# Sliding-window attention by whole chunks: the order of scores, transposes and weighing, and the PSUM banks they use

## The chip, the cores and the metric

The kernel runs on one core of one Trainium2 chip. The metric is the device time of one execution in microseconds. The core's engines work side by side, each through its own instruction queue in order: TensorE (PE; its weight loads are shown apart as PEld), VectorE (DVE), ScalarE (ACT), GpSimd (POOL) and SyncE (SP), which issues most of the DMAs. Matmul results go to PSUM, which has eight banks of 2 KB for each of 128 partitions: one bank holds 128x512 numbers of 32 bits.

## The reference, cut to what matters

The reference computes one layer of a streaming encoder in float32, on 1024 prompt tokens and 64 sample tokens: a projection, retention and sliding-window attention side by side, their merging, cross attention to 256 memory tokens, and a feed-forward block. The change lies in the sliding-window attention. Queries come in chunks of 64; each chunk sees its own 64 keys and the 128 before them. There are 16 query heads and 2 heads of keys and values; each query head has a learned sink, which joins the softmax's denominator.

```python
def swa_attend(q, k, v, bias, sinks, valid):
    s = jnp.einsum('bnqhgd,bnkhd->bnhgqk', q, k, preferred_element_type=jnp.float32) * (SWA_HD ** -0.5)
    s = s + bias.astype(jnp.float32)
    if valid is not None:
        s = jnp.where(valid, s, NEG_INF)
    sink = sinks.astype(jnp.float32)[:, :, None, None]
    m = jnp.maximum(jnp.max(s, axis=-1, keepdims=True), sink)
    e = jnp.exp(s - m)
    p = e / (jnp.sum(e, axis=-1, keepdims=True) + jnp.exp(sink - m))
    return jnp.einsum('bnhgqk,bnkhd->bnqhgd', p.astype(v.dtype), v)
```

One other product of the layer is worked on at the same time: the retention branch's output product, `rms_norm(ret_o) * silu(ret_g)` times `w_ret_out`.

## The kernel before, in words

**Where the change lies.** The projections, the retention and the memory's keys and values come first (up to about 809 us of the profile's clock). Then `swa_phase` runs the attention over 17 chunks (16 of the prompt, one of the sample), from 809 to about 990 us; `merge_swa`, cross attention and the feed-forward block follow and are not touched.

**A chunk's steps.** A chunk c is worked on in two halves hf of eight query heads each. One half has four units (v, i): v is the head of keys and values, i one of two groups. Keys and queries of v=0 lie in partitions 0 to 63, those of v=1 in 64 to 127. `keys(c)` tells how many keys a chunk has: 64 for chunk 0, 128 for chunk 1, 192 for the others.
- `scores(c, hf)`: four matmuls (L972; eight records in the trace) that use half of PE's rows each, into one tile of two PSUM banks, "s", of which there is one. VectorE adds the bias and takes the minimum for each unit (L982, result `nm`), ScalarE takes the exponentials with their sums (L988) and the sinks' exponentials (`es`, L990), VectorE makes the denominators (L991) and reciprocals (L992), and POOL normalises: the first 128 keys in place in tile `t` (L994), the last 64 into tile `e` (L999).
- `turn(c, hf)`: in the first half, `values` transposes up to three blocks of 128 values on PE (L949) into one of the two PSUM banks "d" of the product below, and ScalarE copies each out (L951); a block once transposed is kept for the chunks that follow. Then four transposes of `t` (L1011) into the bank "pt0", copied out by ScalarE (L1015), and two of `e` (L1022) into the bank "pt1", copied out by VectorE (L1024).
- `weigh(c, hf)`: only in the second half, eight matmuls (L1035; sixteen records) of values by transposed weights, into the two banks "out". VectorE copies the result (L1039, `osb`), and every second chunk SP stores it.

**The work in between.** PE is kept busy by the retention's output product: `filler` yields half pieces of it. It first finishes the memory's values (four halves of 256 columns, operands `ms`; ScalarE takes each result out of bank "d", L1167) and then does 24 pieces of `w_ret_out` by `ret`, with 384, 384 or 320 columns. A half piece is twelve matmuls (L156 to L158: three for each of four blocks, since each float32 operand is split into a high and a low part). The splits are made by ScalarE (cast of the high part, L123) and VectorE (the low part, L124; L1120 for the first piece's operands, in `first_low`). `later_operands` loads and splits the retention output's second and third columns while the first pieces run; `marks` holds the `es` instructions that these casts and subtractions are set behind. VectorE multiplies each finished piece by its gate (L1196), and SP stores it.

**What sets the order.** The loop at L1047 emits, for each half, the weighing of the half before, the scores of the half two ahead, the transposes of this half, and then as many half pieces as `fill` names: none before the first step, six after the second, then 38 spread over 34 steps, and eight at the end. `in_order` (`issue_after(self.last_mm)`) sets each part behind the last matmul emitted, and so fixes PE's order; what the other engines do is put in order by a scheduler, which works from its own estimates of times. PSUM: "s" 2 banks, "pt0" 1, "pt1" 1, "out" 2, "d" 2, which is all eight.

Of the kernel before, what the change touches and what calls it, by code (L numbers as in the profile page):

```python
# [11 lines left out]
F32 = mybir.dt.float32  # L12
# [7 lines left out]
P = 128  # L20
# [16 lines left out]
NKEY = 192  # L37
# [72 lines left out]
class Kernel:  # L110
# [816 lines left out]
    def swa(self, ctx, fill):  # L927
        nc, tc, io = self.nc, self.tc, self.io
        if True:
# [26 lines left out]
            halves = [(c, hf) for c in range(17) for hf in range(2)]  # L956
# [7 lines left out]
            def scores(c, hf):  # L964
                ks, j0, nk = keys(c)
                if hf == 0 and c % 4 == 0 and 0 < c < 13:
                    self.load_queries(qTs, c + 4)
                qT = qTs[c // 4 % 2]
                pss = pw.tile([P, 2, 512], F32, tag="s", name="pss")
                for i in range(2):  # L970
                    for v in range(2):
                        self.last_mm = mm(pss[:, v, i * NKEY:i * NKEY + nk], qT[rows[v], 2 * hf + i, c % 4, :],  # L972
                                          kT[rows[v], ks:ks + nk], start=True, stop=True).ins
# [3 lines left out]
                ps = pss[:, :, :2 * NKEY].rearrange("p v (i n) -> p v i n", n=NKEY)  # L977
                bs = bias.rearrange("p (v h i) n -> p v h i n", v=2, h=2)
                nm = sw.tile([P, 2, 2], F32, tag="nm", name="nm")
                for v, i in units:  # L980
                    u = quad(self.minus)[:, v, i:i + 1]
                    nc.vector.tensor_tensor_reduce(t[:, v, i, :nk], ps[:, v, i, :nk], bs[:, v, hf, i, j0:], -0.125, u,  # L982
                                                   ALU.add, ALU.min, nm[:, v, i:i + 1])
# [19 lines left out]
            def turn(c, hf):  # L1003
                ks, j0, nk = keys(c)
                if hf == 0:
                    live[c] = [values(ks + k0) for k0 in ((0, 64, P) if nk == NKEY else (0,))]
                (t, e), vt = live.pop((c, hf)), live[c]
                n = min(P, nk)
                pp = pw.tile([P, 512], F32, tag="pt0", name="pp")
                for j, (v, i) in enumerate(units):  # L1010
                    self.last_mm = nc.tensor.transpose(pp[:n, j * P:(j + 1) * P], t[:, v, i, :n], self.ident).ins  # L1011
                if hf == 0:
                    live[c, "T"] = [self.pw2.tile([P, 2, 512], F32, tag="pT0", name="pT"), self.pw2.tile([P, 512], F32, tag="pT1", name="pT")]
                pT = live[c, "T"][0][:n]
                nc.scalar.copy(pT[:, :, hf * 256:(hf + 1) * 256], pp[:n, :].rearrange("p (v i) -> p v i", v=2))  # L1015
                cs = [slice(h * 256, (h + 1) * 256) for h in range(2)]
                parts = [[(h, v, vt[0][:n], pT[:, v, cs[h]]) for h in range(2) for v in range(2)]]
                if nk == NKEY:
                    pp = pw.tile([P, 512], F32, tag="pt1", name="pp")
                    for i in range(2):  # L1020
                        x = e[:, i].rearrange("p r k -> p (r k)")
                        self.last_mm = nc.tensor.transpose(pp[:, i * P:(i + 1) * P], x, self.ident).ins  # L1022
                    pT = live[c, "T"][1]
                    nc.vector.tensor_copy(pT[:, hf * 256:(hf + 1) * 256], pp[:, :256])  # L1024
                    parts.append([(h, r ^ h, vt[2 - r][rows[r]], pT[rows[r], cs[h]]) for h in range(2) for r in (h, 1 - h)])
                live[c, "parts"] = parts

            def weigh(c, hf):
                if hf == 0:
                    return  # L1030
                parts = live.pop((c, "parts"))
                po = pw.tile([P, 2, 512], F32, tag="out", name="pout")
# [14 lines left out]
            n = len(halves)  # L1047
            for i in range(-2, n):
                if i > 0:
                    self.in_order(lambda: weigh(*halves[i - 1]))  # L1050
                if i + 2 < n:
                    self.in_order(lambda: scores(*halves[i + 2]))
                if i >= 0:
                    self.in_order(lambda: turn(*halves[i]))
                for pieces in next(fill):
                    self.in_order(lambda: next(pieces, None))
                if i == -2:
                    with tc.high_priority(), tc.issue_after(self.last_operand):
                        self.tokens(vT, 1, "cvT")
                if i == 2:  # L1060
                    with tc.issue_after(self.last_operand):
                        self.load_queries(qTs, 4)
                if i == 8:
                    with tc.issue_after(self.last_operand):
                        keep()
            self.in_order(lambda: weigh(*halves[n - 1]))
            for pieces in next(fill):
                self.in_order(lambda: next(pieces, None))
# [765 lines left out]
```

## Time and profile before

| what | before |
|---|---|
| time, median of 3 runs (lowest, highest) | 2181.74 us (2180.3, 2183.03) |
| the profiled execution's own time | 2183.19 us |
| its span | 2181.1 us |
| mean granted clock of PE | 0.995 |
| PE busy, of the span | 2142.3 us (98%) |
| VectorE / ScalarE / POOL busy | 1553.4 / 876.4 / 651.7 us |
| PE busy in 826 to 870 us | 41.58 of 44.00 us |
| PE busy in 890 to 970 us | 80.00 of 80.00 us |

The busy time of PE is close to the span, so the table by itself does not tell what a change of order is worth: that depends on the few stretches in which PE waits, and on how quickly its matmuls follow one another. A row of the timeline holds the start and the duration of a group of like instructions in microseconds; in brackets stands the engine's idle time before it, and what ended that. Matmuls are pipelined: a row's duration is longer than the distance to the next row's start, and the distances are what counts.

### The profile page before, as it was taken

The page shows a single profiled execution, that of the slowest core. Times are in us where ns is not written, and L with a number is a line of the kernel's source. Part 1 is how long each engine was busy: PE and PEld are TensorE (multiplying, and loading weights), DVE is VectorE, ACT ScalarE, POOL GpSimd, SP SyncE. Part 2 cuts the span into 40 slices and gives each one's busy share as a digit, 9 for nine tenths or more (in the row PEclk, how much of TensorE's full clock was granted, in tenths as well). Part 3 has the DMA queues.
Part 4 walks back from the last instruction along what each step waited for, and adds up shares of the span by engine and source line. Part 5 has one row for each costly group of instructions (what it writes and reads, how often), then busy time and mean ns, then how long its engine had stood idle before and what let it go on. Part 6 is the DMA issues. An engine that isn't in the chain of part 4 may idle for free. (4 is left out here: it accounts for less than half of the span.)

```text
span 2181.1 us, 41848 instructions
## 1 busy us (share of the span) xinstructions
PE 2142.3 (98%) x16389; PEld 2089.0 (96%) x16389; DVE 1553.4 (71%) x2824; ACT 876.4 (40%) x1898; POOL 651.7 (30%) x498
## 2 busy tenths in 40 slices
PE   8999999999999999999999999999999999999997
PEld 8999999999999997889999999999999999999997
DVE  8996868776687658665455555768777777787688
ACT  7344424344344447553233333333322322344343
POOL 1223233342344214430000000014565555514531
PEclk9999999999999999999999999999999999999999
DMA  6434354435344467326443111422333323294433
GB/s 208 154 131 114 114 152 125 137 111 159 103 160 164 166 206 246 118 80 219 124 155 120 40 49 59 146 87 91 121 124 116 105 96 120 94 331 128 135 107 119
DMA packets 181446, 290.84 MB, mean 133 GB/s; under 512 B 40290, under 2 KB 109314, under 8 KB 181250
## 3 DMA queue, kind: packets, MB, share of 16 engines
q1 hardware_dynamic: 176130, 278.18, 40.1%
q10 hardware_dynamic: 4608, 8.36, 1.0%
q8 instruction: 129, 2.11, 0.4%
q0 software_dynamic: 512, 1.64, 0.2%
q14 instruction: 67, 0.55, 0.1%
HBM read 196.95 MB, written 91.16 MB: 132 GB/s over the span
## 5 line engine op out<-in xcount | busy, mean ns | idle before, releaser
L124 DVE TENSOR_TENSOR wq<-raw,wq 128x512 fp32r<-128x512 f32 (+1 forms) x499 | 443.9, 893 | 134.8 <-ACT wq L123 131.4
L123 ACT CAST wq<-raw 128x512 fp32r<-128x512 f32 (+1 forms) x499 | 303.1, 614 | 567.1 <-PE pq L215 223.3
L212 PE MATMUL pq<-T,wq 128*128 128x272 f32 x1832 | 492.0, 288 | 4.9 <-ACT wq L123 3.3
L213 PE MATMUL pq<-T,wq 128*128 128x272 f32 x1832 | 492.9, 289 | 0.0
L213 PE MATMUL pq<-B,wq 128*128 128x272 f32 x1592 | 428.2, 289 | 2.9 <-DVE B L124 2.6
L212 PE MATMUL pq<-B,wq 128*128 128x272 f32 x1592 | 426.6, 288 | 0.5 <-ACT B L123 0.5
L190 POOL TENSOR_TENSOR raw<-raw 128x512 f32<-128x512 f32 (+1 forms) x59 | 86.0, 1458 | 1036.5 <-DVE rs_r L301 483.0
L215 PE MATMUL pq<-T,wq 128*128 128x272 f32 x1832 | 382.8, 289 | 1.5 <-DVE wq L124 1.5
L212 PEld LDWEIGHTS pq<-T,wq 128*128 128x128 f32 x1832 | 345.0, 188 | 6.7 <-ACT wq L123 3.1
L213 PEld LDWEIGHTS pq<-T,wq 128*128 128x128 f32 x1832 | 344.9, 188 | 1.2 <-issue 1.1
L215 PE MATMUL pq<-B,wq 128*128 128x272 f32 x1592 | 332.2, 289 | 0.0
L213 PEld LDWEIGHTS pq<-B,wq 128*128 128x128 f32 x1592 | 299.5, 188 | 4.3 <-DVE B L124 4.2
L212 PEld LDWEIGHTS pq<-B,wq 128*128 128x128 f32 x1592 | 299.4, 188 | 1.4 <-ACT B L123 0.9
L215 PEld LDWEIGHTS pq<-T,wq 128*128 128x128 f32 x1832 | 290.2, 190 | 2.6 <-DVE wq L124 1.8
L215 PEld LDWEIGHTS pq<-B,wq 128*128 128x128 f32 x1592 | 252.2, 190 | 0.5 <-issue 0.4
L259 DVE TENSOR_TENSOR u<-pq,u 128x544 f32<-128x544 f32 x177 | 127.2, 719 | 95.5 <-PE pq L215 95.4
L193 POOL TENSOR_TENSOR raw<-raw 128x512 f32<-128x512 f32 (+1 forms) x59 | 80.8, 1370 | 91.4 <-DVE wq L124 81.5
L598 DVE TENSOR_TENSOR stage<-pq,u 128x544 f32<-128x544 f32 x112 | 80.3, 717 | 36.9 <-PE pq L215 32.4
L191 POOL TENSOR_TENSOR raw<-raw 128x512 f32<-128x512 f32 (+1 forms) x59 | 88.8, 1505 | 3.6
L196 POOL TENSOR_TENSOR raw<-raw 128x512 f32<-128x512 f32 (+1 forms) x59 | 84.0, 1423 | 4.4
L1483 POOL TENSOR_TENSOR stage<-stage,rstd_f 128x544 f32<-128x544 f32 x40 | 63.9, 1607 | 39.1 <-ACT stage L1482 39.1
L156 PE MATMUL pd<-xc,wq 128*128 128x256 f32 (+1 forms) x256 | 74.5, 291 | 0.0
(383 smaller groups left out, 4548.4 us busy)
## 6 DMA issues: line engine op xcount, KB each, us to landing
hl<-d_op SPq DMA_DIRECT2D x85, 272.0 KB, 5.3
d_qkv<-stage SPq DMA_DIRECT2D x44, 272.0 KB, 2.7
d_op<-stage SPq DMA_DIRECT2D x44, 272.0 KB, 2.1
d_op<-ht SPq DMA_DIRECT2D x44, 272.0 KB, 3.3
raw<-w_gate SPq DMA_DIRECT2D x22, 512.0 KB, 3.6
raw<-w_up SPq DMA_DIRECT2D x22, 512.0 KB, 4.0
raw<-w_down SPq DMA_DIRECT2D x16, 512.0 KB, 4.8
d_gate<-stage ACTq DMA_DIRECT2D x28, 272.0 KB, 3.0
```

Source lines behind the costliest of these rows:

```text
L123: self.last_cast = self.nc.scalar.copy(hi, src).ins
L124: return self.nc.vector.tensor_tensor(out=lo, in0=src, in1=hi.bitcast(F32), op=ALU.subtract).ins
L156: mm(ps, wh, xh, start=start, stop=False)
L190: tt(out=a11, in0=a11, in1=a21, op=sub)
L191: tt(out=a21, in0=a21, in1=a22, op=add)
L193: tt(out=a11, in0=a22, in1=a11, op=sub)
L196: tt(out=a12, in0=a12, in1=a11, op=sub)
L212: mm(ps[:, c, :HC], w[:, 0, ks], x[:, 0, cs], start=start, stop=False)
L213: mm(ps[:, c, :HC], w[:, 0, ks], x[:, 1, cs], start=False, stop=False)
L215: self.last_mm = mm(ps[:, c, :HC], w[:, 1, ks], x[:, 0, c * HC:(c + 1) * HC], start=False, stop=stop).ins
L259: add = lambda out, a, b: nc.vector.tensor_tensor(out=out, in0=a, in1=b, op=ALU.add)
L598: nc.vector.tensor_tensor(out=o, in0=ps, in1=sb, op=ALU.add)
```

## The change

- `scores(c)` does both halves of a chunk, one behind the other (`half_scores`). Each half's scores go into two tiles of one bank each instead of one tile of two banks. Tag "s" now has four such banks.
- `turn(c)` does the whole chunk: the values' transposes, then the four transposes of `t` of each half, in a fixed order (`most`), each into one bank that it takes from "s" by turns with the scores; ScalarE copies each out. The four transposes of `e` go into the unused upper halves of the two banks "out" that the weighing will write, and VectorE copies all of them out in one instruction.
- `weigh(c)` uses these same two banks.
- The loop goes over chunks: weighing of chunk c-1, scores of chunk c+1, half pieces, transposes of chunk c, half pieces. The empty first step of `fill` goes; the numbers of half pieces stay. The loads of the next queries and the stores of the kept keys and values move to chunk steps.
- PSUM: "s" 4 banks, "out" 2, "d" 2.

In the compiled order this makes a chunk on PE: weighing (c-1), sixteen score records (c+1), one half piece or more, value transposes, eight transposes, four small transposes, one half piece or more. On ScalarE it is: eight exponentials (c+1) and the sinks', casts, value copies, two copies of transposes. In chunk 0 seven of `later_operands`' casts stand before its first copy of transposes and one between the two; in chunk 1 four casts and two weight casts stand before both; in chunk 2 four casts stand before the copies of the value transposes, of which that chunk has two. On SP's queue, the load of the queries of chunks 4 to 7 stands behind four loads for `later_operands` and one store of a piece, where it stood before them.

```diff
-                yield []
                 yield [pieces] * 6
...
-            def scores(c, hf):
+            def scores(c):
+                if c % 4 == 0 and 0 < c < 13:
+                    self.load_queries(qTs, c + 4)
+                for hf in range(2):
+                    half_scores(c, hf)
+
+            def half_scores(c, hf):
                 ks, j0, nk = keys(c)
...
-                pss = pw.tile([P, 2, 512], F32, tag="s", name="pss")
+                pss = [pw.tile([P, 512], F32, tag="s", bufs=4, name="pss") for v in range(2)]
...
-            def turn(c, hf):
+            def turn(c):
                 ks, j0, nk = keys(c)
+                vt = [values(ks + k0) for k0 in ((0, 64, P) if nk == NKEY else (0,))]
                 n = min(P, nk)
+                first = self.pw2.tile([P, 2, 512], F32, tag="pT0", name="pT")[:n]
                 cs = [slice(h * 256, (h + 1) * 256) for h in range(2)]
+
+                def most(hf):
+                    pp = pw.tile([P, 512], F32, tag="s", bufs=4, name="pp")
+                    t = live[c, hf][0]
+                    for j, (v, i) in enumerate(units):
+                        self.last_mm = nc.tensor.transpose(pp[:n, j * P:(j + 1) * P], t[:, v, i, :n], self.ident).ins
+                    nc.scalar.copy(first[:, :, cs[hf]], pp[:n, :].rearrange("p (v i) -> p v i", v=2))
+
+                for hf in range(2):
+                    self.in_order(lambda: most(hf))
+                po = pw.tile([P, 2, 512], F32, tag="out", name="pout")
+                for hf, i in units if nk == NKEY else ():
+                    x = live[c, hf][1][:, i].rearrange("p r k -> p (r k)")
+                    self.last_mm = self.in_order(lambda: nc.tensor.transpose(po[:, hf, (2 + i) * P:(3 + i) * P], x, self.ident)).ins
...
                 if nk == NKEY:
-                    pp = pw.tile([P, 512], F32, tag="pt1", name="pp")
...
-                    nc.vector.tensor_copy(pT[:, hf * 256:(hf + 1) * 256], pp[:, :256])
...
+                    rest = self.pw2.tile([P, 512], F32, tag="pT1", name="pT")
+                    nc.vector.tensor_copy(rest.rearrange("p (h i) -> p h i", h=2), po[:, :, 256:])
...
-            for i in range(-2, n):
-                if i > 0:
-                    self.in_order(lambda: weigh(*halves[i - 1]))
-                if i + 2 < n:
-                    self.in_order(lambda: scores(*halves[i + 2]))
-                if i >= 0:
-                    self.in_order(lambda: turn(*halves[i]))
...
+            self.in_order(lambda: scores(0))
+            with tc.high_priority(), tc.issue_after(self.last_operand):
+                self.tokens(vT, 1, "cvT")
+            filled()
+            for c in range(17):
+                if c:
+                    self.in_order(lambda: weigh(c - 1))
+                if c < 16:
+                    self.in_order(lambda: scores(c + 1))
+                filled()
+                self.in_order(lambda: turn(c))
+                filled()
+                if c == 1:
+                    with tc.issue_after(self.last_operand):
+                        self.load_queries(qTs, 4)
```

More of the change, by code (lines that the diff above doesn't have):

```diff
@@ L955, in swa @@
             units = [(v, i) for v in range(2) for i in range(2)]
-            halves = [(c, hf) for c in range(17) for hf in range(2)]
             live, outs = {}, {}
@@ new lines, in turn, with weigh @@
+                parts = [[(h, v, vt[0][:n], first[:, v, cs[h]]) for h in range(2) for v in range(2)]]
+                if nk == NKEY:
+                    rest = self.pw2.tile([P, 512], F32, tag="pT1", name="pT")
+                    nc.vector.tensor_copy(rest.rearrange("p (h i) -> p h i", h=2), po[:, :, 256:])
+                    parts.append([(h, r ^ h, vt[2 - r][rows[r]], rest[rows[r], cs[h]]) for h in range(2) for r in (h, 1 - h)])
+                live[c] = parts, po
+            def weigh(c):
+                parts, po = live.pop(c)
```

44 lines of the change are left out of this document (8 added, 36 removed).

## The prediction

> **What bounds the kernel now.** I read the page first (busy time by engine), then the windows around the attention stage, then the timelines of PE, ACT and DVE there. The first fence is the page's busy line; then rows of the windows (columns: stretch, its length, busy time and count by engine, granted clock, DMA share, GB/s); then rows of the PE timeline (start, duration, what, idle before it and its releaser).
>
> ```profile
> PE 2142.3 (98%) x16389; PEld 2089.0 (96%) x16389; DVE 1553.4 (71%) x2824; ACT 876.4 (40%) x1898; POOL 651.7 (30%) x498
> ```
>
> ```profile
> 25.00:30.00 5.00, 3.14 (x23) 2.92 (x23) 5.00 (x9) 5.00 (x10) 0.00 (x0) 1.00 0.01 2
> 48.00:50.00 2.00, 1.86 (x13) 1.86 (x14) 2.00 (x4) 1.41 (x4) 1.17 (x1) 0.88 1.02 383
> 50.00:52.00 2.00, 2.00 (x10) 2.00 (x10) 2.00 (x4) 2.00 (x5) 0.00 (x0) 0.50 0.16 45
> 52.00:53.00 1.00, 1.00 (x6) 1.00 (x6) 1.00 (x3) 0.54 (x1) 0.00 (x0) 0.54 0.77 241
> ...
> 808.00:812.00 4.00, 2.17 (x20) 1.73 (x19) 2.52 (x11) 3.43 (x7) 0.02 (x1) 0.83 0.84 258
> 812.00:816.00 4.00, 4.00 (x20) 3.97 (x19) 0.00 (x0) 3.98 (x8) 1.61 (x3) 0.50 0.61 227
> 816.00:820.00 4.00, 4.00 (x30) 4.00 (x29) 2.04 (x12) 3.56 (x20) 0.61 (x1) 0.81 0.20 79
> 826.00:870.00 44.00, 41.58 (x304) 33.95 (x304) 37.37 (x140) 33.12 (x119) 17.96 (x23) 1.00 0.80 263
> ```
>
> ```profile
> 48.14 0.39 PE L212 MATMUL pq<-T,wq 128*128 128x272 f32 x1 [2.42 <-ACT wq L123]
> ...
> 809.31 0.66 PE L972 MATMUL pss<-swin,swin 64*128 64x64 f32 x8 [0.82 <-DVE stage L598]
> 810.99 1.12 PE L972 MATMUL pss<-swin,swin 64*128 64x64 f32 x8 [1.01 <-DVE nm L982]
> 812.03 0.58 PE L156 MATMUL pd<-wq,ms 128*128 128x256 f32 x1
> ...
> 820.27 0.44 PE L156 MATMUL pd<-ret,wq 128*128 128x384 f32 x1
> ...
> 825.28 0.71 PE L972 MATMUL pss<-swin,swin 64*128 64x128 f32 x8
> ...
> 838.59 0.92 PE L972 MATMUL pss<-swin,swin 64*128 64x192 f32 x8 [1.40 <-DVE nm L982]
> ```
>
> PE is busy 98% of the span, so only PE's own time can be won. In the attention stage its idle time is the 0.82 and 1.01 us at the start and 44.00 - 41.58 = 2.42 us from 826 to 870, the largest piece the 1.40 us in which the scores' only buffer waits for VectorE. The clock falls to half twice: from 49.5 to 52.9 (0.48 + 2.00 + 0.92 us at half), after 2.42 us of idle time, and for 1.36 + 4.00 + 1.52 = 6.9 us from 810.6, after 0.82 us and most of the 1.01 us. After 1.86 us of idle time in 25 to 30 it stayed at 1.00. So about 1.5 to 2 us of idle time close together may halve it for 3.4 us, which costs 1.7 us of work.
>
> **Product and switches in a settled chunk.** The PE timeline of one chunk, from its weighing to the next; rows with the same line are the same group seen from a later start:
>
> ```profile
> 871.13 1.68 PE L1035 MATMUL pout<-pT,swin 128*64 128x256 f32 x16
> 872.74 0.92 PE L972 MATMUL pss<-swin,swin 64*128 64x192 f32 x8
> 873.17 0.49 PE L972 MATMUL pss<-swin,swin 64*128 64x192 f32 x4
> 873.33 0.33 PE L972 MATMUL pss<-swin,swin 64*128 64x192 f32 x2
> 873.75 0.60 PE L1011 MATMUL pp<-ident,t 128*128 128x128 f32 x4
> 874.19 0.38 PE L1022 MATMUL pp<-ident,e 128*128 128x128 f32 x2
> 874.33 0.42 PE L156 MATMUL pd<-ret,wq 128*128 128x384 f32 x1
> ...
> 876.15 0.33 PE L157 MATMUL pd<-ret,wq 128*128 128x384 f32 x1
> 876.32 0.34 PE L158 MATMUL pd<-ret,wq 128*128 128x384 f32 x1
> 876.59 0.92 PE L972 MATMUL pss<-swin,swin 64*128 64x192 f32 x8
> 877.44 0.66 PE L1011 MATMUL pp<-ident,t 128*128 128x128 f32 x4
> 877.94 0.38 PE L1022 MATMUL pp<-ident,e 128*128 128x128 f32 x2
> ...
> 880.33 1.68 PE L1035 MATMUL pout<-pT,swin 128*64 128x256 f32 x16
> ```
>
> A chunk takes 880.33 - 871.13 = 9.20 us with no idle time. A further product matmul would have stood at 876.32 + 0.17 = 876.49 (0.17 is 876.15 to 876.32); the transposes follow at 877.44. That is 0.95 us for eight records which inside a group take 4 x 0.163 = 0.65 (873.17 to 873.33 is one pair): 0.30 is entering and leaving the mode. The four transposes behind them take 0.50 (877.44 to 877.94) against 0.44 (873.75 to 874.19). Joining the second scores to the first therefore saves 0.30 + 0.05 = 0.35 us. Chunks 1 to 16 have such a second group apart: 16 x 0.35 = **-5.6**. Scores are now followed by product instead of transposes, transposes come after product; no row prices scores before product. From the leaving of 0.15 I take no difference; 0 to 0.15 either way gives 2.4 us both ways. The Trainium skill ("TensorEngine Tiling (Array Packing)", Key Properties) says that changing the tiling mode drains TensorE; the 0.30 above agrees, and merged groups drain less often.
>
> **The other parts on PE.** Scores in single banks, four buffers: the 1.01 us at 810.99 and the 2.42 us of 826 to 870 go: **-2.4** for the latter. The matmuls, transposes and copied elements stay the same in number, save that two VectorE copies of 128x256 become one of 128x512, off PE.
>
> **The start.** ScalarE's rows:
>
> ```profile
> 818.32 0.35 ACT L988 ACTIVATE t<-t,nm 128x64 f32<-128x64 f32 x1 [0.43 <-DVE nm L982]
> ...
> 819.76 0.46 ACT L1167 ACTIVATE swin<-pd,mtok 128x256 f32<-128x256 f32 x1
> ...
> 829.32 1.74 ACT L123 CAST ret<-swin 128x384 fp32r<-128x384 f32 x4
> ...
> 842.47 1.52 ACT L123 CAST ret<-swin 128x320 fp32r<-128x320 f32 x4
> 843.90 1.14 ACT L123 CAST wq<-raw 128x512 fp32r<-128x512 f32 x2
> ...
> 871.58 0.19 ACT L990 ACTIVATE es<-es 128x4 f32<-128x4 f32 x1
> ...
> 874.34 0.46 ACT L988 ACTIVATE t<-t,nm 128x192 f32<-128x192 f32 x1
> 874.79 0.56 ACT L1015 COPY pT<-pp 128x512 f32<-128x512 f32 x1
> ...
> 883.16 0.27 ACT L951 COPY swin<-pd 128x128 f32<-128x128 f32 x1 [2.58 <-PE pd L949]
> ```
>
> The output product's first piece needs a PSUM bank that ScalarE empties at 819.76, behind both halves' exponentials. Without the 0.43 us wait this ends near 819.7 instead of 820.22. The piece then runs its 24 matmuls of 0.17 (4.1 us, plus 0.15 for the switch) without its gaps, and the scores of chunk 1 begin near 824.1 instead of 825.28: **-1.1**. But the memory product before it starts near 810.7 and, if the 0.82 us alone does not halve the clock, needs only 5.5 us (of its 8.24, 812.03 to 820.27, some 5.4 ran at half): it ends near 816.2, and PE waits 3.5 us for ScalarE. That wait costs nothing itself, but halves the clock behind it: about **+1.6**.
>
> **New waits.** In the compiled order ScalarE does, in each chunk, all eight exponentials of chunk c+1, then casts, then the copies that weighing chunk c needs. Take S as the start of the scores. The first exponential came 1.60 after S (872.74 to 874.34); its bank is now complete one matmul sooner, so 1.45. Eight at 0.45 (874.34 to 874.79) and 0.2 for the sinks (871.58) end at S + 5.25. Durations of neighbours overlap by some 0.1 us, so the sums below are upper ends.
> - Chunk 0: seven casts at 0.435, the value copy of 0.27, a copy of 0.56, one more cast, a last copy of 0.56: S + 10.1 at most; I take 0.8 off, since chunk 1 has 128 keys and neighbours overlap. PE is ready at 1.3 (scores, twice 825.28's) + 0.15 + 2.16 (half a piece, 874.33 to 876.49) + 1.1 (transposes) + 2.2 = S + 6.9: **+2.4**.
> - Chunk 1: four casts in 1.43 (842.47 to 843.90), two in 1.14, two copies: S + 8.9 at most; PE, without value transposes, S + 6.8 to 7.1: **+1.7**.
> - Chunk 2: two value transposes share a bank; the second waits for ScalarE's copy of the first, which stands behind four casts: 5.25 + 1.43 + 0.27 = S + 6.95, against PE at 1.5 + 0.15 + 2.16 + 0.16 = S + 3.95: **+3.0**.
> - Later: copies ready at S + 5.25 + 0.27 + 1.12 = 6.65 at most; PE is due at 9.20 - 0.35 - 1.61 (871.13 to 872.74) = 7.25 with pieces of 384 columns, about 6.6 with 320 (24 matmuls shorter by a sixth). About no stall, but chunk 4 has two weight casts of 0.57 in between and some four chunks one: **+1.0** in all. VectorE's single copy of the small transposes comes in the same order of time and hides behind ScalarE's.
>
> The stalls of chunks 0 and 2 exceed 2 us, so each should halve the clock. Behind chunk 0's the slow product only fills chunk 1's stall: 0. Behind chunk 2's: **+1.6**. The Trainium skill ("TensorE: Matmul & The Clock Gate", What's actually happening) puts the drop after at least one idle window of about 3.4 us. By it these stalls would leave the clock alone; the fall at 49.5 after only 2.42 us of idle time speaks against it.
>
> SP's queue: the query load moves behind four gate loads and a store.
>
> ```profile
> swin<-d_gate SPq DMA_DIRECT2D x32, 192.0 KB, 4.9
> ...
> swin<-d_sq SPq DMA_DIRECT2D x4, 1024.0 KB, 7.8
> ```
>
> It lands 7.8 us after issue, some 20 us ahead of chunk 4: 0. The gate loads for chunk 1's casts follow the store of a product piece; with 4.9 us to land they may come up to 1.5 us after ScalarE is ready for them, so 0 to +1.5; I take 0, since the slowed clock delays ScalarE too. The removed empty step and POOL's queue keep their order: 0.
>
> **Sum.** -5.6 - 2.4 - 1.1 + 1.6 + 2.4 + 1.7 + 3.0 + 1.0 + 1.6 = +2.2 us. The profiled execution took 2183.19, so 2185.4 on its footing; it lies 1.45 above the median of 2181.74, on which I forecast **2184.0**.
>
> **Rivals.**
> - Slower: ScalarE becomes the bound of every chunk. The slack is about 0 (320 columns) to 0.6 us; if an exponential took 0.6 instead of 0.45 us with eight in a row, the copies would come 1.2 us later and 14 chunks stall by 0.6 to 1.2, about +9 beyond the sum with some of its 1.0: 2193. It decides from about 0.5 us of lateness. The pitch of 0.45 speaks against it; that no row has eight in a row speaks for it. The same side is reached if each of four waits halves the clock twice over, as at 810.6 (+5 to +7: 2190).
> - No half clock behind the stalls: 2184.0 - 3.2 = 2180.8. For it: the 1.86 us in 25 to 30 went unpunished; against it: 49.5. This is also what the skill's rule gives.
> - Faster: the early stalls do not appear, because VectorE and ScalarE come to chunk 1 with nothing left over: 2184.0 - 7.1 - 1.6 = 2175.3. Against it: the casts stand ahead of the copies in ScalarE's order, whatever the time.
> - The joined groups save nothing (product behind scores pays what the transposes paid, and more): +5.6, 2189.6. It needs the 0.30 to reappear in full.
>
> **How the numbers follow.** Forecast 0.45 (2181 to 2187); no half clock 0.17; faster 0.13; ScalarE bound or more half clock 0.17; no saving 0.08. 0.2% (4.4 us) is about what a measurement tells from no change, so faster means under 2177.4, slower over 2186.1. The faster case gives 0.13 and a little of the second, 0.15; the last two and the forecast's upper edge 0.33; the rest 0.52. The range takes the faster case's upper part and the slower cases' lower: 2176 to 2191.
>
> **What would show it.** Right: scores in groups of 16 records; settled chunks of 8.85 us; PE idle before the weighing of chunks 0 and 1 released by ACT's copy and before a value transpose of chunk 2; half clock behind that; the 1.40 us gone. Wrong: idle time before each weighing, chunks still of 9.2 us, or a clock of 1.00 throughout.

## The result, and the profile after

| | before | changed |
|---|---|---|
| time, median of ten runs each (lowest, highest) | 2182.11 us (2180.18, 2186.7) | 2187.58 us (2183.75, 2190.2) |
| ratio to before (95% interval) | 1 | 1.0021 (1.0013 to 1.003) |
| span of the profiled execution | 2181.1 us | 2185.3 us |

The changed kernel is slower by 0.21%, some 4.6 us (2.8 to 6.6), where 2184.0 against a median of 2181.74, 2.3 us, was forecast. That is just past the 0.2% that the prediction took as the least that can be told from no change. The median of 2187.58 lies inside the range of 2176 to 2191, and above both the upper edge of the forecast's own case (2187) and the 2186.1 from which the prediction counted a time as slower. A second set of runs of the same changed kernel gave 1.0026 (1.0017 to 1.0035).

Two executions also differ in parts that the change does not touch. The code before and behind the attention stage took between 805 and 810 us up to the first scores, and 1180 to 1185 us from the merging to the end, in the thirteen profiles of this study. So the stage is compared by itself: from the first scores of chunk 0 to the start of the weighing of chunk 16, which in before and in the changed kernel is (PE's timeline, one row of each):

```profile
983.64 1.08 PE L1035 MATMUL pout<-pT,swin 128*64 128x256 f32 x8
```

```profile
982.92 0.87 PE L1037 MATMUL pout<-pT,swin 128*64 128x256 f32 x6
```

With the first scores at 809.31 and 805.67 that is 174.3 us before and 177.3 us after. PE's timeline of the changed kernel shows where the stage waits:

```profile
805.67 1.11 PE L974 MATMUL pss<-swin,swin 64*128 64x64 f32 x16 [0.82 <-DVE stage L598]
...
813.93 0.45 PE L156 MATMUL pd<-ret,wq 128*128 128x384 f32 x1 [1.27 <-ACT swin L1171]
...
818.29 1.16 PE L974 MATMUL pss<-swin,swin 64*128 64x128 f32 x16
...
826.41 0.65 PE L1037 MATMUL pout<-pT,swin 64*64 64x256 f32 x4 [1.53 <-ACT pT L1016]
827.30 0.65 PE L1037 MATMUL pout<-pT,swin 64*64 64x256 f32 x4 [0.24 <-ACT pT L1016]
...
837.05 1.13 PE L1037 MATMUL pout<-pT,swin 128*64 128x256 f32 x8 [0.75 <-ACT pT L1016]
...
841.80 0.27 PE L948 MATMUL pd<-ident,swin 128*128 128x128 f32 x1
845.79 0.47 PE L948 MATMUL pd<-ident,swin 128*128 128x128 f32 x1 [3.72 <-ACT swin L950]
```

Scores come in groups of sixteen records, and VectorE's waits at 810.99 and 838.59 are gone. In their place PE waits for ScalarE: at the weighing of chunk 0 (1.53 + 0.24 us), of chunk 1 (0.75), and before the second value transpose of chunk 2 (3.72). What ScalarE does meanwhile (its timeline, the changed kernel):

```profile
822.73 2.99 ACT L123 CAST ret<-swin 128x384 fp32r<-128x384 f32 x7
...
826.25 0.52 ACT L123 CAST ret<-swin 128x384 fp32r<-128x384 f32 x1
826.66 0.59 ACT L1016 COPY pT<-pp 64x512 f32<-64x512 f32 x1
...
844.06 1.52 ACT L123 CAST ret<-swin 128x320 fp32r<-128x320 f32 x4
845.49 0.25 ACT L950 COPY swin<-pd 128x128 f32<-128x128 f32 x1
```

The casts stand straight ahead of the copies that PE waits for. With these waits the clock halves (windows of the changed kernel; the granted clock is the third number from the end):

```profile
826.00:832.00 6.00, 5.35 (x30) 4.07 (x31) 5.96 (x20) 3.03 (x12) 0.03 (x1) 0.72 0.35 112
844.00:852.00 8.00, 6.21 (x25) 6.21 (x25) 4.43 (x7) 3.18 (x10) 4.22 (x6) 0.57 0.88 278
```

A mean clock of 0.72 is 0.28 short of full, so twice 0.28 of the stretch ran at half: 2 x 0.28 x 6 = 3.4 us, and 2 x 0.43 x 8 = 6.9 us in the second row. A settled chunk (PE's timeline):

```profile
872.14 1.68 PE L1037 MATMUL pout<-pT,swin 128*64 128x256 f32 x16 [0.46 <-DVE pT L1029]
873.75 1.57 PE L974 MATMUL pss<-swin,swin 64*128 64x192 f32 x16
875.25 0.44 PE L156 MATMUL pd<-ret,wq 128*128 128x384 f32 x1
...
877.44 0.27 PE L948 MATMUL pd<-ident,swin 128*128 128x128 f32 x1
877.55 1.03 PE L1015 MATMUL pp<-ident,t 128*128 128x128 f32 x8
878.42 0.60 PE L1023 MATMUL pout<-ident,e 128*128 128x128 f32 x4
878.84 0.44 PE L156 MATMUL pd<-ret,wq 128*128 128x384 f32 x1
...
881.16 1.68 PE L1037 MATMUL pout<-pT,swin 128*64 128x256 f32 x16
```

It takes 9.02 us where before took 9.20: the scores fell from twice 0.85 to 1.50 us, the value transpose from 0.16 to 0.11, the eight transposes from 0.94 to 0.87; but the four small transposes rose from 0.27 to 0.42. The half pieces took 4.51 us (2.19 behind the scores, 2.32 behind the small transposes), against twice 2.26 in before.

### The profile page after: what moved, and what is told of

Read it like the earlier page. It is cut to its first block, busy times and chain, and to the rows that moved or that the text cites. A ratio compares the mean times of both kernels' runs of the same rounds, so it can differ in the third digit from the quotient of the medians.

```text
span 2185.3 us, 41827 instructions
## 1 busy us (share of the span) xinstructions
PE 2140.6 (98%) x16389; PEld 2093.8 (96%) x16389; DVE 1561.4 (71%) x2809; ACT 873.2 (40%) x1898; POOL 652.6 (30%) x498
## 5 line engine op out<-in xcount | busy, mean ns | idle before, releaser
L124 DVE TENSOR_TENSOR wq<-raw,wq 128x512 fp32r<-128x512 f32 (+1 forms) x499 | 449.8, 905 | 155.6 <-ACT wq L123 153.7
L989 ACT ACTIVATE t<-t,nm 128x192 f32<-128x192 f32 (+2 forms) x136 | 58.8, 434 | 60.9 <-DVE nm L983 60.9
```

Of the source, the lines that this page charges most:

```text
L124: return self.nc.vector.tensor_tensor(out=lo, in0=src, in1=hi.bitcast(F32), op=ALU.subtract).ins
```

## The experiments

In this table the stage runs from the first scores to the last weighing in the one profile of each run; waits are PE's in chunks 0, 1, 2, whatever engine ended them; "half" is time at half clock within the stage. Ratios are to before, on the same chip.

| run | waits in chunks 0, 1, 2 (us) | half (us) | stage (us) | ratio (95% interval) |
|---|---|---|---|---|
| before (as shown) | see the prediction | 6.8 | 174.3 | 1 |
| rep_before | the same | 0 | 171.9 | 1.000 (0.999 to 1.0011) |
| changed kernel (as shown) | 1.8, 0.8, 3.7 | 10.3 | 177.3 | 1.0021 (1.0013 to 1.003) |
| rep_after | 1.8, 2.3, 3.7 | 3.4 | 175.8 | 1.0026 (1.0017 to 1.0035) |
| e_casts | 2.2, 0, 4.4 | 6.8 | 175.9 | 1.0014 (1.0005 to 1.0023) |
| e_vbank | 1.8, 2.3, 0.6 | 6.8 | 174.9 | 1.000 (0.9989 to 1.0011) |
| e_order | 0, 3.2, 1.2 | 6.8 | 180.0 | 1.0043 (1.0031 to 1.0055) |
| e_late | 0, 1.3, 3.4 | 6.8 | 173.9 | 1.0009 (0.9998 to 1.002) |
| e_late0 | 0, 1.2, 3.3 | 3.4 | 173.0 | 1.0008 (0.9997 to 1.002) |
| e_busy | 0.5, 2.3, 0 | 3.4 | 175.5 | 1.0011 (1.0001 to 1.0022) |
| e_nocasts | 0, 0, 1.6 | 0 | 168.3 | 0.9989 (0.9976 to 1.0001) |
| e_apart | 0, 0, 2.0 | 0 | 172.5 | 1.0002 (0.9992 to 1.0012) |
| e_pool | 0, 0.4, 1.6 | 0 | 168.8 | 0.9979 (0.9969 to 0.9988) |

The 200.4 and 203.6 us in some expectations run to a later matmul of the merging (at 1009.75 and 1009.31), not to its first; by the marks of the table they are 174.3 and 177.3.

**The two kernels again.** No edit.

> The changed kernel again. The attention stage, from the first scores to the first matmul of the merging (L156 of merge_swa), took 200.4 us in the profile of before (809.31 to 1009.75) and 203.6 us in that of the change (805.67 to 1009.31). Theory A (the stage is slower by itself: ScalarE's copies stand behind casts in chunks 0, 1 and 2, and the clock halves behind these waits): again three waits for ScalarE of about 1.8, 0.8 and 3.7 us, one or two half-clock intervals in the stage, its length 201 to 205 us, the time 1.002 of before. Theory B (the stage is no slower, the time comes from half-clock intervals elsewhere that differ from run to run): a stage of 199 to 201 us, and a ratio that may be 1.000.

> The kernel before again, for a second profile. If its stage repeats: 174.3 us from the first scores to the last weighing, within 2 us, with waits for VectorE at the second scores of chunks 0 and 2 (1.0 and 1.4 us); if the half clock at its start (6.8 us) was chance, its memory product takes 5.5 us instead of 8.2 and the stage up to 2 us less, and what differs elsewhere (before 809 us, behind 1010 us) shows how much of a difference between two single profiles is not the change's.

The changed kernel's waits come back, its half clock does not in full. Rows of rep_after, PE's timeline and windows:

```profile
839.50 1.13 PE L1037 MATMUL pout<-pT,swin 128*64 128x256 f32 x8 [2.31 <-ACT pT L1016]
...
848.24 0.33 PE L948 MATMUL pd<-ident,swin 128*128 128x128 f32 x1 [3.72 <-ACT swin L950]
```

```profile
826.00:832.00 6.00, 4.19 (x33) 2.80 (x32) 6.00 (x10) 3.75 (x10) 2.49 (x2) 1.00 0.43 133
846.00:852.00 6.00, 3.76 (x18) 3.76 (x19) 4.47 (x8) 3.63 (x12) 4.46 (x6) 0.73 0.85 252
```

Behind chunk 0 the clock stayed at 1.00; so chunk 1's weighing, no longer covered by slow product, waited 2.31 instead of 0.75 us, as the prediction's trade between the two has it. In rep_before the stage's start, with the same two waits, kept the full clock, where the first profile of before had it at half for 6.8 us:

```profile
810.63 0.66 PE L972 MATMUL pss<-swin,swin 64*128 64x64 f32 x8 [1.01 <-DVE nm L982]
```

```profile
812.00:816.00 4.00, 4.00 (x36) 4.00 (x35) 0.90 (x9) 3.54 (x14) 0.54 (x1) 1.00 0.45 170
```

Theory A stands: the means of the two profiles are 173.1 and 176.5 us, so the stage itself is 3.4 us longer. Theory B (only chance elsewhere) falls with it, and with two ratios clear of 1. Whether the 1 to 2 us between these 3.4 and the 4.6 to 5.7 of the ratios are the change's can't be told: 3.4 lies inside the first interval and just below the second (3.7).

**One bank for a chunk's value transposes.**

```diff
-                    pt = self.dense_psum()
-                    self.last_mm = nc.tensor.transpose(pt[:n, :P], vT[:, lo:lo + n], self.ident).ins
+                pt = self.dense_psum()
+                for j, lo in enumerate(los):
+                    n = min(P, KC - lo)
+                    self.last_mm = nc.tensor.transpose(pt[:n, j * P:(j + 1) * P], vT[:, lo:lo + n], self.ident).ins
```

> The value transposes of a chunk go side by side into one bank, so that the second doesn't wait for ScalarE's copy of the first; nothing else changes, the casts stand where they stood. Theory A: the 3.7 us in chunk 2 become a wait of about 0.8 us at that chunk's weighing, the waits of chunks 0 and 1 stay (1.8 and 0.8 us), the half-clock interval behind chunk 2 goes (it cost up to 3.4 us), the one behind chunk 0 stays: the stage 197 to 200 us, the time 3 to 6 us under the changed kernel's. Theory B: within 2 us of the changed kernel's.

PE's timeline of this run:

```profile
818.38 0.44 PE L156 MATMUL pd<-ret,wq 128*128 128x384 f32 x1 [2.60 <-ACT swin L1180]
...
843.05 1.97 PE L1046 MATMUL pout<-pT,swin 128*64 128x256 f32 x8 [2.28 <-ACT pT L1025]
853.60 0.65 PE L1046 MATMUL pout<-pT,swin 128*64 128x256 f32 x4 [0.59 <-ACT pT L1025]
```

The 3.72 us became 0.59 at the weighing, as expected, and the time went down from 1.0026 to 1.000 of before. The half clock behind chunk 2 is gone, but here it fell behind chunk 1's 2.28 us, and behind the start, where PE waits 2.60 us for ScalarE to empty a bank. So taking away the wait in chunk 2 alone won back about as much as the whole loss; the stage is shorter by 0.9 to 2.3 us than in the two profiles of the change, and the rest of the gain in time is not seen in a single profile.

**The casts a chunk earlier, and the casts behind the copies.** In e_casts:

```diff
-        a, b = self.marks[-1]
+        a, b = self.marks[-3]
```

> The casts and subtractions of the retention's later columns are set behind the sinks' exponentials one chunk earlier, so that six of the eight casts of chunk 0 stand before the exponentials of chunk 1, and none stand before the value copies of chunk 2. Theory A: the waits of the first two weighings (1.8 and 0.8 us) go, the one between the value transposes of chunk 2 falls from 3.7 to about 1.5 us (its copy stands behind eight exponentials alone), and at least one of the two half-clock intervals goes: the stage 196 to 199 us, the time 4 to 8 us under the changed kernel's. Theory B: the time stays within 2 us of the changed kernel's. Theory C (the joined scores and the new banks slow the settled chunks): the early waits go, but the chunks from the fourth on keep the time above that of before.

Half of this came. Chunk 1's wait went and chunk 2's grew, to 4.43 us; chunk 0's did not go (2.2 us). There the casts now stand ahead of the exponentials and between them, and ScalarE waits for the loads of two of them, 0.77 and 1.35 us (one row of its timeline), so the exponentials and with them the copies come later:

```profile
824.24 0.51 ACT L123 CAST ret<-swin 128x384 fp32r<-128x384 f32 x1 [1.35 <-DMA swin<-d_gate]
```

```profile
846.08 0.47 PE L948 MATMUL pd<-ident,swin 128*128 128x128 f32 x1 [4.43 <-DVE den L992]
```

In chunk 2 the row names VectorE's `den`, but this transpose waits for the bank that ScalarE's copy empties, and that copy ended at the same time (845.78 + 0.24). ScalarE's timeline tells that no cast stood between that chunk's exponentials and the copy; the exponentials themselves began late, since the casts' loads came late (1.96 us) and VectorE did their subtractions before the scores (rows of ACT, and one of DVE):

```profile
839.01 1.75 ACT L123 CAST ret<-swin 128x320 fp32r<-128x320 f32 x4 [1.96 <-DMA swin<-d_gate]
842.17 0.45 ACT L989 ACTIVATE t<-t,nm 128x192 f32<-128x192 f32 x1 [1.41 <-DVE nm L983]
...
845.78 0.24 ACT L950 COPY swin<-pd 128x128 f32<-128x128 f32 x1
```

```profile
840.51 1.28 DVE L124 TENSOR_TENSOR ret<-swin,ret 128x320 fp32r<-128x320 f32 x3
```

The time came out 3 us under that of rep_after (medians 2183.84 and 2186.96), where 4 to 8 were expected.

In e_late and e_late0 the casts and subtractions are set behind the copies of transposes (the loads stay); e_late has the single bank for value transposes too:

```diff
+                    self.last_copy = nc.scalar.copy(first[:, :, cs[hf]], pp[:n, :].rearrange("p (v i) -> p v i", v=2)).ins
...
+        with self.tc.issue_after(self.last_copy):
+            for x, k, c0, n in self.raw_rets:
+                self.split(x, self.rets[k][:, 0, c0:c0 + n], self.rets[k][:, 1, c0:c0 + n])
```

> Two edits on the changed kernel: a chunk's value transposes go side by side into one bank, and the casts and subtractions of the retention's later columns are set behind the chunk's copies of transposes (the loads stay). Measured from the first scores to the last weighing the stage took 174.3 us in before, 177.3 and 175.8 us in two profiles of the change. Theory A (the casts ahead of the copies make the early waits, the waits halve the clock): no wait for ScalarE above 0.6 us in chunks 0 to 2, no half-clock interval there (one may stay behind the first piece, where PE waits for the memory's values): the stage 167 to 171 us, the time 2175 to 2180 us, ratio to before 0.997 to 0.999. If the product then waits for the casts instead (PE idle before the pieces of the second columns, released by VectorE or ScalarE), 2180 to 2183 us.

> As the run before, but with each value transpose in a bank of its own as in the changed kernel: the casts alone are moved behind the copies. Theory A: the waits of the weighings of chunks 0 and 1 go; in chunk 2 the second value transpose waits for the first one's copy behind some four exponentials only, about 0.5 to 1.5 us instead of 3.7; no half-clock interval behind it: the stage 168 to 172 us, the time at most 2 us above that of the run before.

Chunk 0's and chunk 1's weighings no longer wait, as expected; but other waits came. The transposes of chunk 1 wait 1.2 to 1.3 us for VectorE to read the scores, and in e_late0 the second value transpose of chunk 2 still waits 1.56 us. In chunk 2 of e_late, PE's timeline and below it POOL's:

```profile
844.40 0.79 PE L1024 MATMUL pp<-ident,t 128*128 128x128 f32 x4 [2.49 <-POOL t L1002]
846.12 1.11 PE L1024 MATMUL pp<-ident,t 128*128 128x128 f32 x4 [0.93 <-POOL t L1002]
```

```profile
843.31 1.04 POOL L1002 TENSOR_TENSOR t<-t,den 128x512 f32<-128x512 f32 x1 [15.38 <-DVE den L1000]
```

The transposes of chunk 2 wait for POOL's normalising, and that for VectorE's denominators; with these 2.49 + 0.93 us the clock halves again. This is a third place, which neither expectation named. The stage is shorter than the changed kernel's by 2 to 4 us and not shorter than before's, and the ratios are 1.0009 and 1.0008 where 0.997 to 0.999 was expected.

**The casts left out, and the casts on POOL.**

```diff
-                    if step in extra:
-                        i, j = extra.pop(step)
-                        self.later_operands(*CH[i], halves[j])
...
-                for ps in self.pieces(u, rets, c0, n):
+                for ps in self.pieces(u, rets, CH[0][0], n):
```

> The changed kernel without the loads, casts and subtractions of the retention's second and third columns: every piece of the product uses the first columns' operands. Theory A: without the casts no wait for ScalarE above 0.7 us in chunks 0 to 2 and no half-clock interval behind them: the stage to the last weighing 166 to 171 us, the time 2174 to 2179 us. A rival (eight exponentials in a row make the copies late by themselves): waits of 1 us or more stay before the first weighings and at the value transposes.

PE's timeline:

```profile
833.84 1.13 PE L1037 MATMUL pout<-pT,swin 128*64 128x256 f32 x8
...
840.49 0.33 PE L948 MATMUL pd<-ident,swin 128*128 128x128 f32 x1 [1.63 <-ACT swin L950]
```

This kernel leaves out the loads, casts and subtractions of the second and third columns, and so its output is not the layer's. Without this work no weighing waits in chunks 0 and 1, no half clock falls in the stage, and the stage is 7.5 to 9 us shorter than the changed kernel's. The expected bound of 0.7 us missed one place: 1.63 us stay between the value transposes of chunk 2, where the copy stands behind eight exponentials alone. So the rival held for that one wait. e_pool keeps the work, puts the casts on POOL, and has the single bank of e_vbank:

```diff
-                self.split(x, self.rets[k][:, 0, c0:c0 + n], self.rets[k][:, 1, c0:c0 + n])
+                hi, lo = (self.rets[k][:, i, c0:c0 + n] for i in range(2))
+                self.nc.gpsimd.tensor_copy(hi, x)
+                self.nc.vector.tensor_tensor(out=lo, in0=x, in1=hi.bitcast(F32), op=ALU.subtract)
```

> The changed kernel with a chunk's value transposes in one bank, and the casts of the retention's second and third columns on POOL instead of ScalarE (VectorE's subtractions stay). Measured from the first scores to the last weighing: before 174.3 us, the change 177.3 and 175.8, without these casts 168.3. Theory A (ScalarE's casts are what the first weighings wait for): no wait for ScalarE above 0.7 us in chunks 0 to 2, the stage 166 to 170 us, the time 2174 to 2178 us, ratio to before 0.996 to 0.999. A rival: a cast takes POOL 0.7 us or more, so that the sixteen of them hold up POOL's normalising or VectorE's subtractions; then the transposes or the second columns' pieces wait for POOL or VectorE, and the stage is 171 us or more.

PE's timeline, then POOL's casts as a group (shortest, median and longest in ns), then a row of VectorE:

```profile
836.24 1.13 PE L1046 MATMUL pout<-pT,swin 128*64 128x256 f32 x8 [0.42 <-ACT pT L1025]
...
842.58 0.63 PE L1024 MATMUL pp<-ident,t 128*128 128x128 f32 x4 [0.73 <-POOL ret L1144]
...
846.61 1.68 PE L1046 MATMUL pout<-pT,swin 128*64 128x256 f32 x16 [0.88 <-DVE pT L1038]
```

```profile
L1144 POOL CAST ret<-swin x16: 447/502/963, 818.5 to 842.4; 128x384 fp32r<-128x384 f32 x8, 128x320 fp32r<-128x320 f32 x8
```

```profile
842.01 0.41 DVE L990 CUSTOM_DVE_ANT_0 t<-pss,swin,minus 128x192 f32<-128x192 f32 x1
```

A cast takes POOL 0.50 us in the median, hardly more than ScalarE (0.48 in the changed kernel), though four of the sixteen took 0.71 to 0.96 us. PE's weighings wait for ScalarE 0.42 us at most. The ratio is 0.9979 (0.9969 to 0.9988): faster than both kernels, by 3.5 us in the medians (2177.86 against 2181.34). The rival came in part. At 842.58 the profile names a cast of POOL as what ended 0.73 us of waiting, but these transposes do not read `ret`, and the weights that they read had been normalised by 840.05; VectorE finished reading the scores in the bank that they overwrite at 842.42 (842.01 + 0.41), so the wait is rather VectorE's. The weighings of chunks 2 and 3 wait 0.88 and 0.82 us for VectorE's copy, where that of chunk 3 waited 0.23 in the changed kernel.

**The idle time filled.** e_busy adds transposes that no one reads, ahead of the weighing of chunk 0 (12) and between the value transposes of chunk 2 (28):

```diff
+                for j in range(count):
+                    self.last_mm = self.in_order(lambda: nc.tensor.transpose(spare[:, 0, :P], self.ident, self.ident)).ins
```

> The changed kernel with 12 further transposes of the identity before the weighing of chunk 0 and 28 between the value transposes of chunk 2, which fill 1.3 and 3.1 us of the waits with work that no one needs. The order of ScalarE's casts and copies is as it was. If the half clock is a price of the waits themselves (they make PE idle): no half-clock interval behind chunks 0 and 2, the waits' ends where they were, so the stage to the last weighing 172 to 175 us, the time 1 to 4 us under the changed kernel's. If it comes with the early chunks whatever PE does: the intervals stay and the time is the changed kernel's or up to 2 us longer.

PE's timeline and the windows:

```profile
839.33 1.13 PE L1046 MATMUL pout<-pT,swin 128*64 128x256 f32 x8 [2.29 <-ACT pT L1020]
...
845.81 3.22 PE L1040 MATMUL spare<-ident 128*128 128x128 f32 x28
```

```profile
840.00:844.00 4.00, 4.00 (x23) 3.18 (x22) 4.00 (x14) 1.04 (x5) 0.37 (x1) 0.57 0.57 174
844.00:852.00 8.00, 8.00 (x63) 7.96 (x62) 6.22 (x19) 5.70 (x22) 4.47 (x6) 1.00 0.96 293
```

Where PE was kept busy, behind chunk 2, the clock stayed at 1.00, though ScalarE's order had not changed; it fell behind chunk 1, whose 2.29 us I had not filled. So an expected stage of 172 to 175 became 175.5. The ratio of 1.0011 is below 1.0026, but the intervals overlap: that the filling made the kernel faster is likely and not shown. That the half clock follows idle time, and not these chunks as such, is what the two windows show.

**The order within a chunk.** e_order puts both groups of half pieces behind the transposes; e_apart puts the second half's scores back behind the first group:

```diff
-                filled()
                 self.in_order(lambda: turn(c))
                 filled()
+                filled()
```

```diff
-                    self.in_order(lambda: scores(c + 1))
+                    self.in_order(lambda: half_scores(c + 1, 0))
                 filled()
+                if c < 16:
+                    self.in_order(lambda: half_scores(c + 1, 1))
                 self.in_order(lambda: turn(c))
```

> Both groups of half pieces of a chunk come behind its transposes, so that the transposes follow the scores and ScalarE's copies stand between the exponentials, ahead of the casts. Theory A: no wait for ScalarE above 1 us in chunks 0 to 2, no half-clock interval in the stage, and product no longer follows scores (if that switch cost some 0.15 us a chunk, settled chunks of 384 columns fall from 9.02 to about 8.87 us): the stage 192 to 196 us, the time 2172 to 2177 us where before takes 2182. A rival: transposes straight behind the scores wait for banks that VectorE or ScalarE still empties, 0.5 us or more in every chunk: settled chunks of 9.4 us or more, the stage over 200 us.

> The changed kernel with the scores of the second half behind the first group of half pieces again, straight ahead of the transposes, so that the joining of the two halves' scores alone is undone. If joining saves what the settled chunks show (9.20 before, 9.02 after, 0.2 us a chunk), chunks with two half pieces of 384 columns take 9.2 us or more again (9.4 if my 0.35 was right and something else lost the rest); transposes straight behind scores may also wait for VectorE to empty their bank, some 0.5 us, as when both groups of half pieces came behind them. In the first chunks the copies come behind fewer exponentials and casts, so the early waits shrink. Together: settled chunks 9.2 to 9.7 us, the stage to the last weighing 174 to 180 us.

PE's timeline of e_order in a settled chunk:

```profile
876.39 0.33 PE L948 MATMUL pd<-ident,swin 128*128 128x128 f32 x1
876.86 1.31 PE L1015 MATMUL pp<-ident,t 128*128 128x128 f32 x8
878.00 0.60 PE L1023 MATMUL pout<-ident,e 128*128 128x128 f32 x4
```

The rival was right: the first of the eight transposes starts 0.47 us behind the value transpose, where the changed kernel needs 0.11, and the eight take 1.14 us instead of 0.87. They use by turns the banks that the scores have just filled, and VectorE is still reading them; in chunk 1 that wait is 3.2 us and halves the clock. A settled chunk is 9.50 us. Less these 0.36 + 0.27 us it would be 8.87, that is 0.15 under the changed kernel's 9.02, as expected; but 0.06 of it are the four small transposes (0.36 against 0.42), and the two groups of half pieces run as one here, 4.42 against 4.51 us. So no more than these 0.09 us are left as the price of leaving the scores for product.

In e_apart a settled chunk with pieces of 384 and 320 columns lasts from one of these rows to the other:

```profile
873.61 1.68 PE L1037 MATMUL pout<-pT,swin 128*64 128x256 f32 x16
...
882.53 1.08 PE L1037 MATMUL pout<-pT,swin 128*64 128x256 f32 x8
```

8.92 us, where the changed kernel takes 8.66 (881.16 to 889.82); two pieces of 384 columns give 9.24 against 9.02. So joining saves 0.22 to 0.26 us a chunk. But with the scores apart ScalarE's exponentials come in fours and its copies between them; the early waits shrink to 2.0 us in chunk 2, no half clock falls in the stage, which takes 172.5 us where 174 to 180 were expected, and the time equals before's (1.0002). The change's one measurable gain and its loss come from the same step.

## Why the prediction was right, and where its sizes were off

The forecast was a small loss within the bounds of no change. What happened is a loss of 0.21%, just past these bounds, inside the range. The mechanism was right in its main parts: joined scores and new banks saved some microseconds in the chunks, and ScalarE's copies behind casts cost more than that in the first three. Term by term, with the prediction's number first:

- **Joined scores, -5.6.** Right in kind, mis-sized. A chunk saved 0.18 us in its rows (9.20 to 9.02), 0.22 to 0.26 against e_apart, not 0.35: about -3.5 over 16 chunks. The scores saved 0.20 where 0.30 was forecast, and the large transposes, the value transpose among them, 0.12 where 0.05 was; the four small transposes gave 0.15 back, which the prediction had counted as unchanged. For product straight behind scores I had put no difference in, with bounds of 2.4 us both ways: the half pieces took 4.51 us against 4.52, so none is seen.
- **VectorE's waits from 826 us on, -2.4.** Right for the 1.40 and 0.49 us behind the scores' buffer, and the product's 0.35 us is gone too. The remaining 0.18 us were ScalarE's copy of values, and a wait of this kind stays.
- **The start, -1.1 + 1.6.** The wait for ScalarE came (1.27 and 0.91 us in the two profiles of the change, 2.60 in e_vbank), shorter than the 3.5 forecast, and the half clock behind it in only one of the eleven profiles of the changed kernel and its variants (e_vbank). The rows on which this step rests came from a start at half clock: in rep_before, at full clock, the scores of chunk 1 began 13.5 us after the first scores instead of 16.0. In the changed kernel they began 12.6 and 12.3 us after. So the start came out 1 to 4 us shorter, where 0.5 longer was forecast.
- **New waits, +2.4, +1.7, +3.0.** These three came at the rows named: 1.8, then 0.8 or 2.3, then 3.7 us. That they hang on ScalarE's casts e_nocasts and e_pool show; 1.6 of the 3.7 us hang on the eight exponentials.
- **Later waits, +1.0.** They came to 1.4 us (0.23, 0.18, 0.46, 0.20 and 0.36), but mostly by another path, so the size is luck. Three of the five, 0.89 us, end with VectorE's copy of the small transposes, which the prediction had hidden behind ScalarE's copies. Ahead of the weighing at 872.14 ScalarE's copies had ended at 870.21, while VectorE first did 1.49 us of weight subtractions and copied from 871.32 on. The five are the same within 0.01 us in e_nocasts, so they don't hang on the casts left out there.
- **Half clock, +1.6 behind chunk 2 and 0 behind chunk 0.** With chunk 2's wait it fell in both profiles, for 3.4 and 6.8 us. Behind chunk 0 it fell in one, and chunk 1's wait shrank from 2.3 to 0.8 us, as argued. e_busy shows that the idle time is its cause. (In before, the clock also falls to half at 97.3 us, far ahead of the stage, which the prediction does not list.)
- **Sum, +2.2.** The stage's means differ by 3.4 us, the medians of all runs by 5.5, the ratio says 2.8 to 6.6. With the means of the two profiles of each kernel the terms come to -3.5 - 2.4 - 2.3 (start) + 7.0 + 1.4 + 2.6 and 0.9 (half clock with chunks 2 and 0) = +3.7. So errors of two to three microseconds cancelled: the joined scores saved 2 us less and the half clock cost nearly 2 more, and the start cost nearly 3 less. That the sum came within 1.5 us of the stage's difference is in part luck.

Of the rivals, ScalarE as the bound of every chunk did not come: settled chunks got shorter. Nor did the early waits stay away, or the joined groups save nothing. The case without half clock, which is also what the Trainium skill's rule ("TensorE: Matmul & The Clock Gate", What's actually happening: at least one idle window of about 3.4 us) would give for waits of under 3.4 us, did not come either: 1.77 us in the changed kernel, 2.28 us in e_vbank and 2.29 us in e_busy were followed by half clock.

## What to carry to other kernels

When groups of like work are joined on one engine, read the order that this makes on the others: here eight exponentials in a row, with casts behind them, put ScalarE's copies behind work that could have waited, and a saving of 0.2 us a chunk was paid for with 6 to 8 us of waits in the first three. Moving such work in time (e_casts, e_late) mostly moved the wait to the next engine in the chain; moving it to an engine with room (e_pool) removed most of it: 0, 0.4 and 1.6 us are left. And a wait of 2 us is to be priced with the half clock that can follow, and a difference of a few microseconds between two single profiles is to be checked against a second profile of each.

## What the runs showed of the hardware that had not been expected

- Four transposes in one group into the banks "out" take 0.42 us, where twice two in banks of their own took 0.27. In e_order, straight before product as well, they take 0.36. No run tells why.
- A cast of 128x384 or 128x320 numbers takes POOL 0.50 us in the median of sixteen (0.45 to 0.96), against 0.48 on ScalarE (0.44 to 0.52).

**Where a wait falls decides whether the clock halves.** In each of the thirteen profiles the times at which half clock begins lie whole multiples of 3.413 us apart, which is also how long the shortest of them lasted: in the changed kernel 827.89 and 844.95, 5 x 3.413 apart. So an execution can be cut into stretches of 3.41 us that end at these times. In the attention stage the clock was half behind each of the eleven stretches in which PE was idle for 1.78 us or more while at full clock, and behind only one of those with 1.69 us or less (1.52, in before). The same wait counts in full when it lies in one stretch, and not when it is cut in two:

| wait | stretch of 3.41 us | PE busy, idle in it (us) | clock in the next |
|---|---|---|---|
| changed kernel, chunk 0: 1.77 us | 824.48 to 827.89 | 1.63, 1.78 | 0.50 |
| rep_after, chunk 0: 1.80 us | 824.91 to 828.32 | 2.43, 0.98 | 1.00 |
| e_busy, chunk 1: 2.29 us | 837.16 to 840.57 | 1.24, 2.17 | 0.50 |
| rep_after, chunk 1: 2.31 us | 835.14 to 838.56 | 2.05, 1.37 | 1.00 |
| before, start: 0.82 + 1.01 us | 807.26 to 810.68 | 1.90, 1.52 | 0.50 |
| rep_before, start: 0.81 + 1.01 us | 809.03 to 812.45 | 2.41, 1.01 | 1.00 |

Outside the stage there are exceptions both ways: in before, 0.84 us idle from 93.88 to 97.29 was followed by half clock, and 1.84 us from 2165.77 to 2169.18 was not. The rule is read off these traces, and no run tests it. In the stage half clock lasted one such stretch or two.
